# One table of times for attention, gates and out-product, and logits with a map in each half of the rows

## The chip, the core and the metric

The kernel runs on one core of a Trainium2 chip. Such a core has TensorE (PE, matrix products; its loads of weights are listed apart as PEld), VectorE (DVE), ScalarE (ACT), GpSimd (POOL) and SyncE (SP, which here only issues DMAs). Data lies in DRAM, in SBUF (128 partitions) or in PSUM (128 partitions in banks of 512 float32, where products are summed). The metric is the device time of one launch in microseconds (us).

## What is computed

The reference is one layer of an encoder over 1024 rows of width 1024, batch 1, in float32. The two groups of heads share one input projection; their results, side by side, go through one output projection, and an MLP follows.

```python
h = rms(x, norm1_g[l])
p = h @ w_in[l]
...
mix_a = mlstm_group(qk_m, v, o, gates, gate_b[l], mlstm_norm_g[l])   # 4 heads x 128
mix_b = diff_attention_group(qa, ka, va, ...)                        # 4 heads, 2 maps x 64
x = x + concat(mix_a, mix_b) @ w_out[l]
u = square(relu(rms(x, norm2_g[l]) @ w_ff1[l]))
x = x + u @ w_ff2[l]
```

Group A ends with its gate: `sigmoid(o) * hs`, where `o` is a projection of h and hs the normed scan. Group B is differential attention, with two maps of 64 dimensions for each head:

```python
q = rms(q, q_g) * 64**-0.5; k = rms(k, k_g)        # per map m = 0, 1
logits[m] = q[m] @ k[m].T + bias                     # T5 relative bias
pr = softmax(logits)
a = pr[0] - lam * pr[1]                              # 1024 keys
out = rms(a @ v, sub_g) * (1 - lam_init)
```

## The kernel before

Products that need more than one rounding are split: a float32 operand becomes a high part (`hi`, the copy by ACT in the type fp32r) and a low part (`lo`, the rest, by DVE or POOL), and `mm3` adds up three matmuls (lines 158 to 160): hi x hi, lo x hi, hi x lo. A full matmul here is 128 rows deep and 512 columns wide and fills one PSUM bank.

The program goes through stages: projections, the mLSTM of group A (its order on PE, DVE, ACT and POOL is written out by a table `O` of times, in units of work on PE: each piece of code is put on a heap with a time, and the pieces are recorded in the order of their times), then attention, the output projection, and the MLP. The change concerns the attention stage and what runs beside it.

Attention goes through 32 items. An item is one head and one block of 128 queries; the first 16 items are the first half of the rows (4 heads x 4 blocks), the other 16 the second half. Every four items, `att_load` brings a head's q and k (POOL's queue), a row table of the bias (`toe`) and v (SP's queue). For an item, `att_logits` makes for each map a tile `pl` of 128 x 1024 in PSUM (L947); DVE adds the bias, moves it to SBUF and finds the row minimum in one instruction (the signs are turned; L952); ACT takes the exponential (L955). `att_weights` mixes the maps (L962 to L965) and turns the result on PE in eight 128 x 128 transposes into two tiles `pa` (L970), which DVE and ACT copy (L973, L975). `att_product` sums eight matmuls with v into `pav` (L985; the trace has two records for each), and ACT, POOL and DVE norm it (L987 to L991). `att_turn` turns four items at once back into columns (L998).

A pl tile has two buffers in PSUM (two banks each), `pa` two, `pav` one, and `pw`, which holds gates and out-product tiles, one.

The logits: the q of a head in SBUF has its high part in the rows 0 to 63 and again in the rows 64 to 127 (two copies, two DMAs), and the same for its low part; k has its high part in the rows 0 to 63 and its low part in the rows 64 to 127. One matmul of 128 rows thus adds two of the four terms; two matmuls (q hi, q lo) make all four, for each of two maps and two halves of the keys: eight matmuls an item.

Between the items stand two generators, taken a step at a time by `step()` at a rate: `output_gates()` (L885 on: for four heads and two halves 24 matmuls into `po`, then DVE, ACT tanh, DVE with the scan's result `mfo` read back from DRAM, ACT and POOL for the split `mm`, a store) up to item 14, and `out_product(0)` from item 18 (eight tiles `pw0` of 24 matmuls, with weights split by ACT and POOL). At item 14 the buffers of the gates are given up and those of the out-product taken. The scheduler of the framework orders the instructions of this stage on each engine: it estimates when operands and engines are free, and may put a matmul of a generator anywhere between those of an item. `mfo`, `so` and `mm` have one buffer each.

The weights of the first two gates, `raw_o`, are split inside `output_gates()`, by DVE. The half 1 of the out-product and the MLP follow behind the stage.

Of the kernel before, what the change touches and what calls it, by code (L numbers as in the profile page):

```python
# [16 lines left out]
P = 128  # L17
# [31 lines left out]
def hybrid_block_kernel(ctx: ExitStack, tc: tile.TileContext, xT, w_v, w_kg, w_c, w_va, w_qa, w_o, w_1, w_2, vec, rel, onehot, outT):  # L49
# [11 lines left out]
    k_dram = [[tc.dram_tile([2, 64, 2, HB], F32, name=f"k_dram{h}{g}") for g in range(2)] for h in range(NH)]  # L61
    q_dram = [[tc.dram_tile([64, 2, 2, HB], F32, name=f"q_dram{h}{g}") for g in range(2)] for h in range(NH)]
# [103 lines left out]
    wturn = [0]  # L166

# [156 lines left out]
    def head_turn(pool, tag, bufs, z, g, is_q):  # L324
# [5 lines left out]
        for h in range(NH):  # L330
# [219 lines left out]
    def qa_done(t, p):  # L550
# [29 lines left out]
        WV=4.86, DF=0.3, Z0=1.48, Z1=2.48, Z2=2.99, Z3=5.34,  # L580
# [28 lines left out]
    for t, x in need:  # L609
        if x in W:  # L610
            continue
        late = max(t + (O["V0"] + (x - 8) * O["WV"] if x >= 8 else 0), late)
        when(late + O["W0"], w_room, x)

        first = t + max(x - 8, 0) - 0.6
        when(min(late + O["W1"], first), w_hi, x)
        when(min(late + O["W2"], first), w_lo, x)

# [266 lines left out]
    def output_gates():  # L885
        for h in range(NH):
            whi, wlo = wsplit(w_c[8 + h], f"o{h}", nc.vector if h < 2 else nc.gpsimd)
            for g in range(2):
                sl = slice(g * HB, (g + 1) * HB)
                p = psB.tile([P, HB], F32, tag="pw", name=f"po{h}{g}")  # L890
                for k in range(KT):
                    kt = slice(k * P, (k + 1) * P)
                    mm3(p, whi[:, kt], wlo[:, kt], hhi[k][:, sl], hlo[k][:, sl], k == 0, k == KT - 1)
                    if k == 3:
                        yield
                mf = spool.tile([P, HB], F32, tag="mf", name=f"mfo{h}{g}")
                loaded[0] = nc.sync.dma_start(mf, mf_dram[h][g]).ins
                so = spool.tile([P, HB], F32, tag="so", name=f"so{h}{g}")
                nc.vector.tensor_tensor(so, p, rb[:, sl], op=ALU.mult)
                nc.scalar.activation(so, so, AF.Tanh, scale=0.5)  # L900
                nc.vector.scalar_tensor_tensor(so, so, 1.0, mf, op0=ALU.add, op1=ALU.mult)
                mm = spool.tile([P, 2, HB], F32R, tag="mm", name=f"mm{h}{g}")
                nc.scalar.activation(mm[:, 0], so, AF.Copy)
                nc.gpsimd.tensor_tensor(mm[:, 1], so, mm[:, 0].bitcast(F32), op=ALU.subtract)
                nc.gpsimd.dma_start(mx_dram[h][g], mm.bitcast(F32))
                yield

# [12 lines left out]
    def att_load(it):  # L920

        h, half, hd = it.h, it.half, it.head
        hd.q = tpool.tile([P, 2, 2, HB], F32R, tag="q", name=f"q{half}{h}", bufs=2)
        for r in range(2):
            nc.gpsimd.dma_start(hd.q[r * 64 : r * 64 + 64], q_dram[h][half])
        hd.kk = tpool.tile([P, 2, S], F32R, tag="kk", name=f"kk{half}{h}", bufs=2)
        for g in range(2):
            nc.gpsimd.dma_start(
                hd.kk[:, :, g * HB : (g + 1) * HB], k_dram[h][g].rearrange("i p m t -> (i p) m t")
            )  # L930
        hd.toe = tpool.tile([P, NTOE], F32, tag="toe", name=f"toe{half}{h}", bufs=2)
        first = h * 2048 + 128 * (4 - 4 * half)
        nc.sync.dma_start(hd.toe, bass.AP(tensor=bt_dram.tensor, offset=bt_dram.offset + first, ap=[[1, P], [1, NTOE]]))
        hd.v = tpool.tile([P, NC, P], F32, tag="v", name=f"v{half}{h}", bufs=2)
        nc.sync.dma_start(hd.v, va_dram[:, :, h * P : (h + 1) * P].rearrange("c p v -> p c v"))

    def att_logits(it):

        h, qi, qb, hd = it.h, it.qi, it.qb, it.head
        it.sm = sm = tpool.tile([P, 8], F32, tag="sm", name=f"sm{qb}{h}", bufs=4)  # L940
        it.l = []
        for m in range(2):
            pl = psB.tile([P, S], F32, tag="pl", name=f"pl{qb}{h}{m}", bufs=2)
            for i in range(2):
                for kh in range(2):
                    sl = slice(kh * HB, (kh + 1) * HB)
                    nc.tensor.matmul(  # L947
                        pl[:, sl], hd.q[:, m, i, qi * P : (qi + 1) * P], hd.kk[:, m, sl], start=i == 0, stop=i == 1
                    )
            lt = tpool.tile([P, S], F32, tag=f"l{m}", name=f"l{qb}{h}{m}", bufs=3)  # L950
            off = 128 * (3 - qi)
            nc.vector.tensor_tensor_reduce(  # L952
                lt, pl, hd.toe[:, off : off + S], 1.0, 3.0e38, ALU.add, ALU.min, sm[:, m : m + 1]
            )
            nc.scalar.activation(lt, lt, AF.Exp, bias=sm[:, m : m + 1], scale=-1.0, accum_out=sm[:, 2 + m : 3 + m])  # L955
            it.l.append(lt)

    def att_weights(it):

        h, qb, sm = it.h, it.qb, it.sm  # L960
# [3 lines left out]
        a = it.l[0]  # L964
        nc.vector.scalar_tensor_tensor(a, it.l[1], rc, a, op0=ALU.mult, op1=ALU.add)  # L965
        it.ats = []
        for j2 in range(2):
            pa = psB.tile([P, HB], F32, tag="pa", name=f"pa{qb}{h}{j2}", bufs=2)
            for j in range(4):
# [116 lines left out]
    for _ in range(5):  # L1086
        step()
# [638 lines left out]
```

## Time and profile before

| What | Value |
|---|---|
| median of 3 runs | 1325.01 us (1322.83 to 1330.72) |
| profiled execution, its own time | 1329.64 us |
| its span in the profile | 1327.8 us |
| mean granted clock of PE in it | 0.984 |
| the attention stage in it | 372 to 647 us |

The profiled execution lies 4.63 us above the median of the runs. All times of single instructions come from it. In the profile a busy time is the sum over an engine's instructions; a wait is put down to the instruction whose end released it ("PE pl L947 <- DVE sm L952" reads: PE, at line 947, waited for DVE at line 952). PEclk, the granted clock, is a share of PE's full speed.

### The profile page before, as it was taken

The page shows a single profiled execution, that of the slowest core. Times are in us where ns is not written, and L with a number is a line of the kernel's source. Part 1 is how long each engine was busy: PE and PEld are TensorE (multiplying, and loading weights), DVE is VectorE, ACT ScalarE, POOL GpSimd, SP SyncE. Part 2 cuts the span into 40 slices and gives each one's busy share as a digit, 9 for nine tenths or more (in the row PEclk, how much of TensorE's full clock was granted, in tenths as well). Part 3 has the DMA queues.
Part 4 walks back from the last instruction along what each step waited for, and adds up shares of the span by engine and source line. Part 5 has one row for each costly group of instructions (what it writes and reads, how often), then busy time and mean ns, then how long its engine had stood idle before and what let it go on. Part 6 is the DMA issues. An engine that isn't in the chain of part 4 may idle for free.

```text
span 1327.8 us, 16889 instructions
## 1 busy us (share of the span) xinstructions
PE 1275.1 (96%) x6315; PEld 1056.1 (80%) x6315; DVE 857.4 (65%) x1159; ACT 605.2 (46%) x1033; POOL 281.4 (21%) x281
## 2 busy tenths in 40 slices
PE   8999989998978998999989999999999999999998
PEld 7898667887867887788878688888887888888887
DVE  7534447886327786777467888666665585458754
ACT  5323426775525555555335455445444343333332
POOL 6532312463225345442100000000000000005001
PEclk9999899999999999999999899999999999999999
DMA  6404354454196568551634476345337955344632
GB/s 210 161 24 143 69 153 102 119 134 127 49 288 165 149 209 255 160 137 49 235 138 143 147 242 231 119 153 170 127 118 263 367 182 203 120 151 159 209 132 88
DMA packets 102865, 212.49 MB, mean 160 GB/s; under 512 B 9072, under 2 KB 22128, under 8 KB 101760
## 3 DMA queue, kind: packets, MB, share of 16 engines
q1 hardware_dynamic: 78368, 154.50, 36.4%
q0 software_dynamic: 8128, 25.43, 7.1%
q10 hardware_dynamic: 16288, 31.50, 6.8%
q8 instruction: 49, 0.80, 0.3%
q14 instruction: 32, 0.26, 0.1%
HBM read 153.10 MB, written 58.29 MB: 159 GB/s over the span
## 4 chain that ended last, share of the span: by engine, by line
PE 49%; DVE 5%; ACT 1%; issue 1%; DMA 0%; POOL 0%; ACTq 0%; DVEq 0%; POOLq 0%
PE z L1568 8%; PE z L1566 8%; PE z L1567 8%; PE m L1237 7%; PE m L1238 7%; PE m L1239 7%; PE pw L160 1%; PE pw L158 1%; PE pw L159 1%; PE pav L985 1%; DVE y L1439 1%; ACT l L955 0%; PE pl L947 0%; DMA re<-in_w_dram 0%; PE pa L970 0%
## 5 line engine op out<-in xcount | busy, mean ns | idle before, releaser
L1604 POOL TENSOR_TENSOR zx<-zx,res 128x512 f32<-128x512 f32 x4 | 8.7, 2179 | 504.6 <-DVE zx L1602 504.6
L955 ACT ACTIVATE l<-l,sm 128x1024 f32<-128x1024 f32 x64 | 73.2, 1145 | 60.8 <-DVE sm L952 60.6
L1568 PE MATMUL z<-wbh,wa0l 128*128 128x512 f32 x224 | 87.4, 390 | 0.6 <-DVE wa0l L1157 0.6
L1566 PE MATMUL z<-wbh,wa0h 128*128 128x512 f32 x224 | 87.2, 389 | 0.0
L1568 PE MATMUL z<-weh,wa1l 128*128 128x512 f32 x224 | 87.2, 389 | 0.0
L1567 PE MATMUL z<-wel,wa1h 128*128 128x512 f32 x224 | 87.1, 389 | 0.0
L1567 PE MATMUL z<-wbl,wa0h 128*128 128x512 f32 x224 | 87.1, 389 | 0.0
L1566 PE MATMUL z<-weh,wa1h 128*128 128x512 f32 x224 | 87.1, 389 | 0.0
L952 DVE CUSTOM_DVE_ANT_0 l<-pl,toe 128x1024 f32<-128x1024 f32 x64 | 76.1, 1219 | 4.0 <-PE pl L947 2.2
L947 PE MATMUL pl<-kk,q 128*128 128x512 f32 x256 | 70.3, 412 | 6.9 <-DVE sm L952 6.7
L1286 ACT ACTIVATE sq<-sq 128x512 f32<-128x512 f32 x48 | 30.3, 632 | 91.8 <-DVE sq L1325 69.0
L1157 DVE TENSOR_TENSOR wel<-g,weh 128x1024 fp32r<-128x1024 f32 x28 | 35.2, 1258 | 56.5 <-ACT weh L1154 56.5
L985 PEld LDWEIGHTS pav<-v,at 128*128 128x128 f32 x512 | 62.5, 196 | 11.4 <-DVE at L973 4.9
L1157 DVE TENSOR_TENSOR wbl<-g,wbh 128x1024 fp32r<-128x1024 f32 x28 | 35.4, 1264 | 56.0 <-ACT wbh L1154 56.0
L1154 ACT ACTIVATE weh<-g 128x1024 fp32r<-128x1024 f32 x28 | 29.7, 1060 | 90.2 <-PE z L1568 53.4
L1154 ACT ACTIVATE wbh<-g 128x1024 fp32r<-128x1024 f32 x28 | 29.7, 1061 | 89.9 <-PE z L1568 52.6
L985 PE MATMUL pav<-v,at 128*128 128x128 f32 x512 | 65.5, 282 | 5.2 <-DVE at L973 3.0
L947 PEld LDWEIGHTS pl<-kk,q 128*128 128x128 f32 x256 | 46.9, 193 | 16.7 <-DVE sm L952 7.3
L160 PE MATMUL pw<-mix,lo_wo 128*128 128x512 f32 x128 | 51.8, 404 | 4.6 <-DVE lo_wo L134 4.6
L158 PE MATMUL pj_c<-hhi,hi_c 128*128 128x512 f32 x128 | 54.2, 423 | 0.0
L158 PE MATMUL pw<-mix,hi_wo 128*128 128x512 f32 x128 | 53.0, 414 | 0.2
L159 PE MATMUL pw<-mix,hi_wo 128*128 128x512 f32 x128 | 51.4, 401 | 0.0
(454 smaller groups left out, 3720.7 us busy)
## 6 DMA issues: line engine op xcount, KB each, us to landing
g<-g_dram SPq DMA_DIRECT2D x56, 512.0 KB, 4.1
g_dram<-gs SPq DMA_DIRECT2D x64, 256.0 KB, 4.5
g_dram<-sq ACTq DMA_DIRECT2D x42, 256.0 KB, 2.1
q<-q_dram POOLq DMA_DIRECT2D x16, 512.0 KB, 6.5
kk<-k_dram POOLq DMA_DIRECT2D x16, 512.0 KB, 7.2
raw_wo<-in_w_o_dram SPq DMA_DIRECT2D x16, 512.0 KB, 4.6
re<-in_w_dram SPq DMA_DIRECT2D x16, 512.0 KB, 4.4
ro<-in_w_dram SPq DMA_DIRECT2D x16, 512.0 KB, 3.5
```

Of the source, the lines that this page charges most:

```text
L158: nc.tensor.matmul(out, ahi, bhi, start=start, stop=False)
L947: nc.tensor.matmul(pl[:, sl], hd.q[:, m, i, qi * P : (qi + 1) * P], hd.kk[:, m, sl], start=i == 0, stop=i == 1)
L952: nc.vector.tensor_tensor_reduce(lt, pl, hd.toe[:, off : off + S], 1.0, 3.0e38, ALU.add, ALU.min, sm[:, m : m + 1])
L955: nc.scalar.activation(lt, lt, AF.Exp, bias=sm[:, m : m + 1], scale=-1.0, accum_out=sm[:, 2 + m : 3 + m])
L985: nc.tensor.matmul(pav[:, 0:P], at, it.head.v[:, c], start=c == 0, stop=c == NC - 1)
L1157: nc.vector.tensor_tensor(dst[1][idx], src, dst[0][idx].bitcast(F32), op=ALU.subtract)
L1237: nc.tensor.matmul(p, wh, xh, start=go, stop=False, skip_group_check=True)
L1238: nc.tensor.matmul(p, wh, xl, start=False, stop=False, skip_group_check=True)
L1239: nc.tensor.matmul(p, wl, xh, start=False, stop=stop and k == 3, skip_group_check=True)
L1566: nc.tensor.matmul(p, wh, gh, start=go, stop=False, skip_group_check=True)
L1567: nc.tensor.matmul(p, wh, gl, start=False, stop=False, skip_group_check=True)
L1568: nc.tensor.matmul(p, wl, gh, start=False, stop=end, skip_group_check=True)
```

## The change

It has two parts.

The first is the layout of the logits. q and k of a head now lie with map 0 in the rows 0 to 63 and map 1 in the rows 64 to 127, the high and the low part one behind the other in each row. They are written to DRAM by one DMA of 512 KB instead of two of 256 KB, and q is read once instead of twice. A matmul is now 64 rows deep: for each half of the keys three terms (hi x hi, lo x hi, hi x lo; the product of the low parts is left out), each for map 0 in the upper and for map 1 in the lower half of PE's rows, in turn: twelve matmuls an item. The two maps write to two `pl` tiles, which are both taken when an item's logits begin.

The second is the order. The stage is now recorded from one table `A` with times in units of one item, for PE, DVE, ACT, POOL and SP's queue. The functions of an item are cut into pieces (logits with bias, exponential, weights, transposes, copies, product, square, root, norm, turn, and the loads of q, k, `toe` on one time and v on another). The gates become pieces `gate_unit`, with halves of twelve matmuls one item apart, and the half 0 of the out-product becomes pieces `out_tile`. The split of the first two gate weights moves into the table `O` of the mLSTM stage. `out_product` keeps only the half 1.

```diff
-    k_dram = [[tc.dram_tile([2, 64, 2, HB], F32, name=f"k_dram{h}{g}") for g in range(2)] for h in range(NH)]
-    q_dram = [[tc.dram_tile([64, 2, 2, HB], F32, name=f"q_dram{h}{g}") for g in range(2)] for h in range(NH)]
+    k_dram = [[tc.dram_tile([P, 2, HB], F32, name=f"k_dram{h}{g}") for g in range(2)] for h in range(NH)]
+    q_dram = [[tc.dram_tile([P, 2, HB], F32, name=f"q_dram{h}{g}") for g in range(2)] for h in range(NH)]
...
-            for m in range(2):
-                nc.scalar.dma_start(
-                    dst[h][g][:, m] if is_q else dst[h][g][:, :, m, :].rearrange("i p t -> p i t"),
-                    zz[m * 64 : m * 64 + 64].bitcast(F32),
-                )
+            nc.scalar.dma_start(dst[h][g], zz.bitcast(F32))
...
+    rows_at = begin_at[11]
+    for h in range(2):
+        for x, f in (("R", g_room), ("H", g_hi), ("L", g_lo)):
+            when(rows_at + O[f"G{x}{h}"], f, h)
...
-        hd.q = tpool.tile([P, 2, 2, HB], F32R, tag="q", name=f"q{half}{h}", bufs=2)
-        for r in range(2):
-            nc.gpsimd.dma_start(hd.q[r * 64 : r * 64 + 64], q_dram[h][half])
+        hd.q = tpool.tile([P, 2, HB], F32R, tag="q", name=f"q{half}{h}", bufs=2)
+        nc.gpsimd.dma_start(hd.q, q_dram[h][half])
...
-            for i in range(2):
-                for kh in range(2):
-                    sl = slice(kh * HB, (kh + 1) * HB)
-                    nc.tensor.matmul(
-                        pl[:, sl], hd.q[:, m, i, qi * P : (qi + 1) * P], hd.kk[:, m, sl], start=i == 0, stop=i == 1
-                    )
...
+            it.pl = [psB.tile([P, S], F32, tag="pl", name=f"pl{qb}{h}{x}", bufs=2) for x in range(2)]
+            for kh in range(2):
+                sl = slice(kh * HB, (kh + 1) * HB)
+                for n, (i, j) in enumerate(((0, 0), (1, 0), (0, 1))):
+                    for x in range(2):
+                        r = slice(x * 64, x * 64 + 64)
+                        nc.tensor.matmul(
+                            it.pl[x][:, sl], hd.q[r, i, qi * P : (qi + 1) * P], hd.kk[r, j, sl], start=n == 0, stop=n == 2
+                        )
...
-    pending.append(output_gates())
...
-        step()
-        if 1 < n < 34:
-            att_weights(items[n - 2])
...
+    order.enter_context(tc.manual_schedule(engines={E.PE, E.DVE, E.Activation, E.Pool, E.SP}))
+    A = dict(
+        G0=-0.05, G1=0.219, E0=0.984, E1=1.396, W=1.626, A0=2.667, A1=2.819, C0=2.714, C1=2.824, P=3.534, SQ=3.666,
...
+        when(t + A["PX"], room)
+        when(t, part, 0)
+        when(t + s, part, 4)
+        when(t + s + A["PE"], out)
+        when(t + s + A["PT"], gate)
+        when(t + s + A["PB"], both)
...
+        when(t, part, 0)
+        when(t + A["OS"], part, 4)
+        when(t + A["OS"] + A["OE"], add)
...
+    while table:
+        t, _, f, args = heapq.heappop(table)
+        f(*args)
```

Three places show the new order. The first is the beginning of the stage on SP's queue: the loads of gate weights (`raw_o`), of the scan's results (`mfo`), and of item 0's `toe` and v. Before:

```order
L131 DMA raw_o_3606<-in_w_c_dram 128x1024
L131 DMA raw_o_3954<-in_w_c_dram 128x1024
L897 DMA mfo_3326<-mf_dram_82 128x512
L933 DMA toe_3291<-bt_dram 128x1408
L935 DMA v_3293<-va_dram 128x8x128
L897 DMA mfo_3361<-mf_dram_83 128x512
L933 DMA toe_3430<-bt_dram 128x1408
```

Now:

```order
L926 DMA toe_3288<-bt_dram 128x1408
L931 DMA v_3290<-va_dram 128x8x128
L1141 DMA mfo_3292<-mf_dram_82 128x512
L1141 DMA mfo_3322<-mf_dram_83 128x512
L1141 DMA mfo_3357<-mf_dram_84 128x512
L1105 DMA raw_o_3391<-in_w_c_dram 128x1024
L926 DMA toe_3435<-bt_dram 128x1408
```

v, which is read from `va_dram`, has moved ahead of the first `mfo`, and the third and fourth gate weights behind the third.

The second place is DVE at the same time, with the gates of the first two units (`so`) and item 0's minimum (`l`, `sm`). Before:

```order
L899 TENSOR_TENSOR so_3328<-po_3301,rb 128x512
L901 SCALAR_TENSOR_TENSOR so_3328<-so_3328,mfo_3326 128x512
L899 TENSOR_TENSOR so_3363<-po_3336,rb 128x512
L901 SCALAR_TENSOR_TENSOR so_3363<-so_3363,mfo_3361 128x512
L952 ISA l_3396,sm_3390<-pl_3391,toe_3291 128x1024
```

Now:

```order
L1145 TENSOR_TENSOR so_3319<-po_3294,rb 128x512
L1149 SCALAR_TENSOR_TENSOR so_3319<-so_3319,mfo_3292 128x512
L1145 TENSOR_TENSOR so_3354<-po_3324,rb 128x512
L950 ISA l_3374,sm_3359<-pl_3360,toe_3288 128x1024
L950 ISA sm_3359 128x1
L950 ISA l_3389,sm_3359<-pl_3361,toe_3288 128x1024
L950 ISA sm_3359 128x1
L1149 SCALAR_TENSOR_TENSOR so_3354<-so_3354,mfo_3322 128x512
```

Item 0's minimum has moved ahead of the second unit's multiplication with `mfo`, and stays behind the first unit's. On PE, the 48 matmuls of the first two gate units stand ahead of item 0's logits.

The third place is PE between the last gate and the first out-product tile (`pw`), in the items 12 to 18. Before:

```order
L947 MATMUL pl_4348<-kk_3947,q_3944 128x512 x4
L947 MATMUL pl_4356<-kk_3947,q_3944 128x512 x4
L970 MATMUL pa_4389<-ident,l_4185 128x128 x4
L158 MATMUL pw_4550<-mix_4309,hi_wo_4319 128x512
L159 MATMUL pw_4550<-mix_4309,hi_wo_4319 128x512
L970 MATMUL pa_4396<-ident,l_4185 128x128 x4
L970 MATMUL pa_4438<-ident,l_4266 128x128 x4
L970 MATMUL pa_4445<-ident,l_4266 128x128
L985 MATMUL pav_4364<-v_3952,at_4338 128x128 x4
L985 MATMUL pav_4364<-v_3952,at_4345 128x128 x4
```

Now (the last two rows stand six times in turn):

```order
L986 MATMUL pav_4143<-v_3799,at_4086 128x128 x4
L986 MATMUL pav_4143<-v_3799,at_4094 128x128 x4
L972 MATMUL pa_4162<-ident,l_3964 128x128 x4
L972 MATMUL pa_4171<-ident,l_3964 128x128 x4
L945 MATMUL pl_4179<-kk_3969,q_3967 128x512
L945 MATMUL pl_4180<-kk_3969,q_3967 128x512
```

An item is now product, transposes and logits, always in this order. In the six steps from item 12 to 18 no matmul of `pw` stands between them; elsewhere twelve matmuls of `po` or `pw` follow the logits in one piece. Behind the stage, from the half 1 of the out-product on, the order on every engine is as before.

More of the change, by code (lines that the diff above doesn't have):

```diff
@@ new lines, in item_pieces, with on @@
+    def item_pieces(n, it):
+        def on(name, f, *args):
+            when(n + A[name], f, it, *args)
+        if n % 4 == 0:
+            when(n + A["LD"] if n else -98.0, att_load, it)
+            when(n + A["LV"] if n else -97.0, att_load_v, it)
+        for m in range(2):
+            on(f"G{m}", att_logits, m)
+            on(f"E{m}", att_exp, m)
+            on(f"A{m}", att_across, m)
+            on(f"C{m}", att_copy, m)
+        on("W", att_weights)
+        on("P", att_product)
+        on("SQ", att_square)
+        on("RS", att_root)
+        on("ON", att_unit)
+        if n % 4 == 3 and n < 31:
+            V = {}
+            when(n + A["TU"], att_turn, items[n - 3 : n + 1], V)
+            when(n + A["TH"], att_hi, it, V)
+            when(n + A["TL"], att_lo, it, V)
@@ L1120, in hybrid_block_kernel @@
+    gate_pieces()
+    when(A["SW"], swap)
+    first_half()
+    for n, it in enumerate(items):
+        item_pieces(n, it)
+    last = {}
+    while table:
+        t, _, f, args = heapq.heappop(table)
+        f(*args)
+    order.close()
     load_mix(1)
```

286 lines of the change are left out of this document (169 added, 117 removed).

## The prediction

> **What bounds the kernel now.** I read the page first, for the span and the share of each engine.
>
> ```profile
> span 1327.8 us, 16889 instructions
> PE 1275.1 (96%) x6315; PEld 1056.1 (80%) x6315; DVE 857.4 (65%) x1159; ACT 605.2 (46%) x1033; POOL 281.4 (21%) x281
> ```
>
> PE is busy for 96% of the span and no other engine comes near it, so time is won only by giving PE less to do or by closing its gaps. The change touches one stage, the attention with the gates and half of the out-product, which the timeline puts at 372 to 647 us. The second view is therefore a table of stretches of that stage. Its columns are the stretch, its length, the busy time of PE, PEld, DVE, ACT and POOL with instructions, PE's granted clock, the DMA share and GB/s.
>
> ```profile
> 372.00:385.00 13.00, 12.22 (x55) 9.46 (x53) 1.53 (x3) 4.46 (x7) 3.49 (x5) 1.00 1.09 328
> 385.00:412.00 27.00, 20.43 (x88) 16.36 (x88) 14.79 (x24) 10.60 (x18) 8.15 (x11) 0.87 0.70 202
> 412.00:433.00 21.00, 17.54 (x95) 14.72 (x95) 14.98 (x27) 9.68 (x19) 10.07 (x14) 0.92 0.75 198
> 433.00:491.00 58.00, 57.56 (x354) 49.59 (x353) 45.79 (x83) 31.80 (x68) 21.93 (x40) 1.00 0.57 161
> 491.00:547.00 56.00, 48.90 (x290) 39.63 (x288) 39.10 (x71) 30.45 (x60) 28.46 (x40) 0.97 0.86 252
> 547.00:647.00 100.00, 96.47 (x583) 82.98 (x584) 72.27 (x124) 50.97 (x101) 32.77 (x52) 1.00 0.41 124
> sum 275.00, PE 253.11 PEld 212.75 DVE 188.46 ACT 137.95 POOL 104.86; mean PE 42.19 PEld 35.46 DVE 31.41 ACT 22.99 POOL 17.48
> ```
>
> PE stands idle for 275 - 253.1 = 21.9 us here, half of the 1327.8 - 1275.1 = 52.7 us of the whole span. The clock is below 1 in three stretches: (1 - 0.87) x 27 + (1 - 0.92) x 21 + (1 - 0.97) x 56 = 6.9 us. Together 28.8 us is what an order without any gap could win. The third view, PE's waits in the same stretch (us in total, times, longest), says what the gaps are.
>
> ```profile
> PE pl L947 <- DVE sm L952: 6.7, 2, 6.4
> PE pa L970 <- ACT at L975: 3.9, 3, 2.4
> PE pav L985 <- DVE at L973: 3.0, 1, 3.0
> PE pt L998 <- DVE on L991: 2.9, 3, 1.7
> ```
>
> They are waits for evictions that came late on an engine that was itself not full, so these are gaps of order, not of capacity.
>
> **The change, part one: the order.** A dense stretch shows what one item (128 queries of one head) costs PE when nothing waits. The columns are the start, the length, and the operation.
>
> ```profile
> 583.86 2.09 PE L947 MATMUL pl<-kk,q 128*128 128x512 f32 x8
> 585.79 1.95 PE L985 MATMUL pav<-v,at 128*128 128x128 f32 x16
> 587.50 0.47 PE L158 MATMUL pw<-mix,hi_wo 128*128 128x512 f32 x1
> 590.33 1.03 PE L970 MATMUL pa<-ident,l 128*128 128x128 f32 x8
> 591.12 2.10 PE L947 MATMUL pl<-kk,q 128*128 128x512 f32 x8
> ```
>
> Matmuls overlap, so I take distances of starts: logits 1.93, product 1.71, twelve matmuls of the out-product 2.83 (0.236 each), transposes 0.79; together 7.26 us. DVE's work for the same item is in the groups of the stage (count, then busy and mean ns of one).
>
> ```profile
> L952 DVE CUSTOM_DVE_ANT_0 l<-pl,toe 128x1024 f32<-128x1024 f32 x64 | 76.1, 1219 | 4.0 <-PE pl L947 2.2 <-DVE on L991 0.5
> L965 DVE SCALAR_TENSOR_TENSOR l<-l,sm,l 128x1024 f32<-128x1024 f32 x32 | 42.7, 1333 | 0.9
> L973 DVE COPY at<-pa 128x512 f32<-128x512 f32 x32 | 21.8, 683 | 2.8 <-PE pa L970 2.8
> L991 DVE TENSOR_SCALAR on<-pav,sm 128x128 f32<-128x128 f32 x32 | 11.2, 349 | 28.2 <-POOL sm L89 28.2
> L963 DVE TENSOR_SCALAR sm<-sm,cst 128x1 f32<-128x1 f32 x32 | 8.6, 271 | 1.0
> ```
>
> That is 2 x 1.22 + 1.33 + 0.68 + 0.35 + 0.27 = 5.07 us, under 7.26 where an item has its twelve matmuls of gate or out-product beside it. The new table gives nearly every item such a group, in one piece. Where it does, I take the gaps to close. Two places of the new order keep gaps.
>
> The first is the start. The gate's chain runs over these rows: the wait and the load of v on SP's queue, the late gate on DVE, the two halves of the split on ACT and POOL, and the sizes and landing times of three loads.
>
> ```profile
> SPq L935 <- DMA va_dram<-z: 14.9, 2, 13.4
> 384.94 0.37 SPq L935 DMA_DIRECT2D v<-va_dram  x1
> 395.27 0.69 DVE L901 SCALAR_TENSOR_TENSOR so<-so,mfo 128x512 f32<-128x512 f32 x1 [9.72 <-DMA mfo<-mf_dram]
> 380.79 0.63 ACT L903 ACTIVATE mm<-so 128x512 fp32r<-128x512 f32 x1 [1.30 <-DVE so L901]
> 381.51 1.28 POOL L904 TENSOR_TENSOR mm<-so,mm 128x512 fp32r<-128x512 f32 x1 [11.97 <-ACT mm L903]
> mfo<-mf_dram SPq DMA_DIRECT2D x8, 256.0 KB, 4.9
> q<-q_dram POOLq DMA_DIRECT2D x16, 512.0 KB, 6.5
> raw_o<-in_w_c_dram SPq DMA_DIRECT2D x4, 512.0 KB, 3.8
> ```
>
> DVE waits 9.72 us for mfo, and item 0's minimum stands behind it; PE's 6.4 us wait is that one. In the new order the first mfo stands behind v on SP, and v waits until va_dram is written. The write competes with 328 GB/s of other traffic. Two gate weights (2 x 0.5 MB) move behind the mfo loads and q is one copy instead of two (0.5 MB less), so 1.5 MB are out of the way: 1.5 MB / 328 GB/s = 4.6 us. So v starts at about 384.9 - 4.6 = 380.3, mfo lands 4.9 + 0.4 later at 385.6, and the chain adds 0.69 + 0.63 + 1.28 + 0.69 = 3.3: PE may go on at 388.9. PE has 48 gate matmuls (11.2 us) and item 0's logits (1.8) from the stage's start at 372 on, to about 385.1. That leaves 3.8 us idle, and I add 2 for a low clock behind it, as the second stretch shows one: 6.
>
> The second is items 12 to 18. The gates have run out, the out-product has not begun, and nothing lies between one item and the next. PE then needs 1.77 (worked out below) + 1.71 + 0.79 = 4.27 us per item, DVE 5.07: PE waits 0.8 six times, 5 us. All of an item's logits now need both psum tiles free, so PE can't run ahead of DVE there. Other stages show what a written table leaves.
>
> ```profile
> 165.00:373.00 208.00, 197.31 (x1093) 166.90 (x1092) 134.32 (x173) 118.05 (x305) 76.06 (x61) 0.98 0.43 116
> 690.00:1327.00 637.00, 630.12 (x2739) 513.23 (x2737) 417.21 (x484) 269.55 (x348) 24.18 (x13) 0.99 0.51 174
> ```
>
> They have 10.7 idle in 208 us and 6.9 in 637, which for 275 us is 14 and 3. My 6 + 5 = 11 lies between; bounds of what stays are 3 and, if nothing closes, 28.8. The order gives 28.8 - 11 = 17.8.
>
> **Part two: the logits.** Before, an item has 8 matmuls with 128 rows, the high and low part of k stacked. Now it has 12 with 64 rows: three terms instead of four (low times low is left out), two maps, two halves of the keys. The two maps take turns in the upper and the lower half of the rows and write to different psum banks. No row of before shows two row halves at work together. The nearest rows are a small tile of 32 rows among full ones.
>
> ```profile
> 167.30 0.40 PE L160 MATMUL pj_c<-hhi,lo_c 128*128 128x512 f32 x1
> 167.62 0.65 PE L372 MATMUL pbt<-oh,rts 32*32 32x512 f32 x2
> 168.20 0.50 PE L158 MATMUL pj_c<-hhi,hi_c 128*128 128x512 f32 x1
> 168.54 0.40 PE L159 MATMUL pj_c<-hlo,hi_c 128*128 128x512 f32 x1
> ```
>
> From 167.30 to 168.54 are four matmuls in 1.24 us, where four full ones at 0.233 take 0.93. So a small matmul costs what a full one does, and the way into another tile size and back costs 0.31 us for both. If the two halves run at once, the logits are six steps: X = 6 x 0.233 + 0.31 + about 0.06 for the second of a pair = 1.77 instead of 1.93, a gain of 0.16 x 32 = 5.1 us. If the change of size costs nothing, X = 1.40 and the gain is 17. If one half waits for the other, X = 12 x 0.233 + 0.37 = 3.17 and 32 x 1.24 = 39.7 are lost. I take the first: 64 rows leave the other half of the array free, and successive matmuls use different halves, weights and banks. The Trainium skill (TensorEngine Tiling, Key Properties) says that different tiles can load weights and multiply in parallel, and that a change of tiling mode drains TensorE; the 0.31 us agrees with the second, and no run of before shows the first.
>
> **Part three: the rest, at nothing.** One DMA of 512 KB on ACT's queue in place of two of 256 KB moves the same bytes. The split of two gate weights moves to the end of the mLSTM stage's table, on the same engines and at nearly the same place; DVE is idle there (1.53 us busy in the first stretch's 13), and if that cover is gone it is two instructions. Splits of gates and of out-product stay on POOL, which is busy 104.9 of 275 us. Behind the stage the order is the same on every engine.
>
> **The sum.** 17.8 + 5.1 = 22.9, so 1329.6 (the profiled execution) becomes 1306.7. This execution lies 4.6 us above the median of the runs, 1325.0; taken off, the forecast is **1302 us**, a ratio of 0.983.
>
> **The rivals.**
>
> First, the halves run one after the other, so that the row halves don't do what they are for. For it speaks that a 32-row matmul costs a full one's time and that nothing before shows an overlap. PE then gets 39.7 us more; the gap of items 12 to 18 vanishes (3.17 + 1.71 + 0.79 = 5.67 is above DVE's 5.07), so 6 us of gaps stay: 1325 - (28.8 - 6) + 39.7 = 1342, **slower**. The point from which it decides is X = 2.5: then 32 x 0.57 = 18 eats the order's gain. Chance 0.18.
>
> Second, the gaps stay. The waits for evictions are only moved: mfo now stands behind v on SP, gate chains have one buffer, and a table holds an engine at a wait even if something behind it could go. Against it: 433 to 491 us shows the same mix at 57.56 of 58 busy. If 24 of the 28.8 us stay, the gain is 4.8 + 5.1 = 9.9: 1315. Chance 0.20.
>
> Third, the halves overlap only in part, because each matmul needs its own weights loaded. The row is
>
> ```profile
> L947 PEld LDWEIGHTS pl<-kk,q x256: 186/188/337, 384.4 to 622.9; 128*128 128x128 f32 x128
> ```
>
> and 12 loads at 0.188 make X = 2.26 + 0.37 = 2.63, a loss of 0.70 x 32 = 22.4. With 7 us of gaps left that is 1325 - 21.8 + 22.4 = 1326. For it: each pair needs two loads. Against it: a load may be shorter with half the rows. Chance 0.12. The Trainium skill (TensorE: Matmul & The Clock Gate, Part 3) says that loads overlap running matmuls only of other row groups, which speaks for this rival; the page's rows here, with PE 96% and PEld 80% busy, show loads under matmuls of the same full tile. The same section measured 3.07 times for four 32-row tiles; at that share of the ideal an estimate by this page is X = 6 x 0.303 + 0.37 = 2.19, and the sum would be 1316.
>
> **How the numbers follow.** My forecast has a chance of 0.50; its own range is 1288 to 1312 (X = 1.40 with 9 us of gaps left below, X = 1.95 with 16 above). About 1% is what a measurement of this kernel can tell from no change, so faster means below 1311.8 and slower above 1338.3. Faster: 0.48 of the forecast's 0.50 and 0.06 of the second rival's 0.20, 0.54. Slower: 0.16 of the first rival, 0.01 of the third, 0.17. Within 1%: the remaining 0.29. The range goes from 1285, where gaps of 3 us and X = 1.50 meet, to 1335, which takes in the second and third rivals and leaves out most of the first.
>
> **What would show it.** In the new profile the start of an item's first logits to the start of its next work should be near 1.77 us in the dense part; 2.6 or 3.2 mean the third or the first rival. The two matmuls of a pair should start almost together. PE should be idle some 4 us at 385 to 389 behind mfo, and 0.8 us per item in items 12 to 18, with the minimum on DVE as releaser; between items elsewhere there should be no gap above 0.5 us. More than 15 us idle in the stage means the second rival. From the out-product's second half on, the distances should equal those of before. I am wrong if X is above 2.2, if SP's v starts later than 384, or if the fillers' groups themselves wait for splits on POOL.

## The result and the profile after

The changed kernel takes 1289.95 us in the median of four runs (1289.83 to 1292.14); the kernel before took 1324.55 us on the same chip (1322.83 to 1330.72). The ratio is 0.9735, with a 95% interval from 0.9701 to 0.9768. The forecast was 1302 us: right in sign and inside its range, 12 us too cautious.

The page of the changed kernel's profile begins so:

```profile
span 1290.4 us, 17143 instructions
PE 1257.0 (97%) x6443; PEld 1038.3 (80%) x6443; DVE 860.0 (67%) x1159; ACT 603.5 (47%) x1033; POOL 272.6 (21%) x273
```

The span is 37.4 us shorter; PE's busy time has fallen by 18.1 of these, and its idle time by the other 19.3, from 52.7 to 33.4. To see where, I read the start of the same work in both traces: the first matmul of the mLSTM's state (`pd`) at 212.0 before and 206.2 now, the first gate matmul (`po`) at 372.2 and 362.3, the first matmul of the MLP (`m`) at 697.6 and 660.8. So 5.8 us were won by the first mark, 4.1 between it and the attention, 26.9 in the attention and out-product, 0.6 behind. The forecast had 22.9 us, all in the attention.

The next view is the table of stretches of the attention in the changed kernel (columns as before: stretch, length, busy PE, PEld, DVE, ACT, POOL, PEclk, DMA share, GB/s).

```profile
362.30:376.30 14.00, 13.22 (x64) 9.88 (x61) 3.30 (x4) 5.36 (x8) 1.88 (x2) 1.00 0.55 178
376.30:455.00 78.70, 78.70 (x508) 64.38 (x507) 63.78 (x112) 43.98 (x88) 30.99 (x48) 1.00 0.58 186
455.00:489.00 34.00, 28.99 (x220) 24.29 (x219) 29.34 (x53) 21.16 (x44) 18.48 (x31) 0.95 0.75 252
489.00:609.00 120.00, 119.34 (x796) 100.24 (x795) 94.61 (x163) 66.91 (x135) 43.50 (x70) 1.00 0.50 163
sum 246.70, PE 240.25 PEld 198.79 DVE 191.03 ACT 137.41 POOL 94.84; mean PE 60.06 PEld 49.70 DVE 47.76 ACT 34.35 POOL 23.71
```

PE is busy all of the 78.7 us behind the start and 119.34 of 120 us at the end. What is left is one stretch, 455 to 489 us, the items without a filling group: 5.0 us idle and 1.7 of a lower clock. PE's waits in it (us in total, times, longest) are these.

```profile
PE pav L986 <- DVE on L1001: 2.9, 3, 1.5
PE pav L986 <- DVE mix L1017: 1.6, 1, 1.6
PE pt L1008 <- DVE on L1001: 0.6, 1, 0.6
```

Most are for the norm `on`, behind which the single `pav` buffer comes free. None is for the minimum, which I had named as the releaser. The start, where I expected PE to wait 3.8 us for a chain behind `mfo`, has only 0.78. The timeline of ACT's and SP's queues, PE and DVE there:

```profile
365.04 0.33 ACTq L845 DMA_DIRECT2D va_dram<-z  x1
...
367.25 0.36 SPq L931 DMA_DIRECT2D v<-va_dram  x1
367.66 12.06 SPq L1141 DMA_DIRECT2D mfo<-mf_dram  x3
...
368.91 0.50 PE L158 MATMUL po<-hhi,hi_o 128*128 128x512 f32 x1 [0.78 <-DVE so L1145]
...
372.26 0.69 DVE L1149 SCALAR_TENSOR_TENSOR so<-so,mfo 128x512 f32<-128x512 f32 x1 [3.40 <-DMA mfo<-mf_dram]
```

v starts 2.2 us after the last write of `va_dram` was issued (9.95 before, from 374.99 to 384.94), and `mfo` is used 4.6 us behind its issue. The gate's chain ended at 375.02, while PE was on item 0's logits (374.70 to 376.29), so the next gate matmul did not wait.

An item in the dense part now looks like this (start, length, operation):

```profile
503.48 1.04 PE L972 MATMUL pa<-ident,l 128*128 128x128 f32 x8
504.45 1.66 PE L945 MATMUL pl<-kk,q 64*128 64x512 f32 x12
506.04 0.51 PE L158 MATMUL pw<-mix,hi_wo 128*128 128x512 f32 x1
506.39 0.40 PE L159 MATMUL pw<-mix,hi_wo 128*128 128x512 f32 x1
506.62 0.40 PE L160 MATMUL pw<-mix,lo_wo 128*128 128x512 f32 x1
...
508.93 1.95 PE L986 MATMUL pav<-v,at 128*128 128x128 f32 x16
510.71 1.04 PE L972 MATMUL pa<-ident,l 128*128 128x128 f32 x8
```

Twelve matmuls of the logits take 1.59 us from the first start to the start of the next work, so they cannot run one behind the other. But the second full matmul behind them starts 0.35 us after the first instead of 0.23, and the eight transposes ahead of them take 0.97 to the next start, where they took 0.79.

### The profile page after: what moved, and what is told of

The parts are those of the page before. It is cut to its first block, busy times and chain, and to the rows that moved or that the text cites. A ratio compares the mean times of both kernels' runs of the same rounds, so it can differ in the third digit from the quotient of the medians.

```text
span 1290.4 us, 17143 instructions
## 1 busy us (share of the span) xinstructions
PE 1257.0 (97%) x6443; PEld 1038.3 (80%) x6443; DVE 860.0 (67%) x1159; ACT 603.5 (47%) x1033; POOL 272.6 (21%) x273
## 4 chain that ended last, share of the span: by engine, by line
PE 83%; DVE 8%; DMA 3%; issue 2%; ACT 2%; POOL 1%; SPq 0%; DVEq 0%; ACTq 0%; POOLq 0%
PE z L1707 8%; PE z L1705 8%; PE z L1706 8%; PE m L1376 7%; PE m L1377 7%; PE m L1378 7%; PE pav L986 4%; PE pl L945 3%; PE pv L235 3%; PE pw L158 2%; PE pa L972 2%; PE pw L160 2%; PE pw L159 2%; PE pj_c L158 2%; PE pj_c L159 2%
## 5 line engine op out<-in xcount | busy, mean ns | idle before, releaser
L945 PE MATMUL pl<-kk,q 64*128 64x512 f32 x384 | 53.3, 408 | 0.0
L159 PE MATMUL pj_c<-hlo,hi_c 128*128 128x512 f32 x128 | 50.7, 396 | 0.0
```

The costliest lines, as they stand in the source:

```text
L159: nc.tensor.matmul(out, ahi, blo, start=False, stop=False)
L945: nc.tensor.matmul(it.pl[x][:, sl], hd.q[r, i, qi * P : (qi + 1) * P], hd.kk[r, j, sl], start=n == 0, stop=n == 2)
```

## The experiments

**The order alone.** The logits go back to the old layout and the eight matmuls of 128 rows; the table stays.

```diff
-                for n, (i, j) in enumerate(((0, 0), (1, 0), (0, 1))):
-                    for x in range(2):
-                        r = slice(x * 64, x * 64 + 64)
-                        nc.tensor.matmul(
-                            it.pl[x][:, sl], hd.q[r, i, qi * P : (qi + 1) * P], hd.kk[r, j, sl], start=n == 0, stop=n == 2
-                        )
...
+                        nc.tensor.matmul(
+                            it.pl[x][:, sl], hd.q[:, x, i, qi * P : (qi + 1) * P], hd.kk[:, x, sl], start=i == 0, stop=i == 1
+                        )
```

> The changed kernel with the old logits (old layout, two q copies, 8 matmuls of 128 rows), the new order kept. If the new order carries the gain and the two row halves run at once, only 32 x (1.93 - 1.78) = 4.8 us of the logits come back: 1295 us, with X near 1.93 and the stage's idle time at or below the 7 us of the changed kernel. If the merged DMAs (one instead of two when q and k are written, one copy of q) carry part of the gain, the start of the stage and the stretch ahead of it also grow again, by 5 to 10 us: 1300 to 1305.

Measured: 1303.64 us (1297.98 to 1304.71), ratio to before 0.9823 (0.979 to 0.9857). The second branch of the expectation, in the time. In the trace the stage from the first `po` to the MLP's first matmul takes 299.7 us, against 325.4 before and 298.5 in the changed kernel: the order is worth 25.7 us and the logits 1.2 by these single executions. The attention starts at 372.4 us, as before. The two stages, up to the end of the out-product's first half (this kernel, then the changed one):

```profile
372.40:629.60 257.20, 251.80 (x1492) 218.68 (x1490) 191.85 (x331) 138.80 (x275) 98.07 (x158) 0.99 0.70 199
362.30:617.50 255.20, 248.75 (x1619) 205.81 (x1617) 191.78 (x331) 138.79 (x275) 94.84 (x151) 0.99 0.56 184
```

Where the logits stand, the changed kernel is 2.0 us shorter. Behind that mark it loses 0.8 again (43.3 us at a granted clock of 0.92, here 42.5 at 0.96), where the order is the same. The same item as above, in the order alone:

```profile
499.89 1.04 PE L978 MATMUL pa<-ident,l 128*128 128x128 f32 x8
500.68 2.10 PE L951 MATMUL pl<-kk,q 128*128 128x512 f32 x8
...
505.38 1.95 PE L992 MATMUL pav<-v,at 128*128 128x128 f32 x16
507.17 1.04 PE L978 MATMUL pa<-ident,l 128*128 128x128 f32 x8
```

From transposes to transposes it needs 7.28 us (499.89 to 507.17), the changed kernel 7.23 (503.48 to 510.71). The row halves win 0.34 us in the logits (1.93 to 1.59) and give back 0.18 ahead of them and 0.10 in the filling group behind: 0.06 an item remain.

**The logits alone.** The kernel before with the new layout and the new matmuls in `att_logits`, its scheduler kept.

```diff
+        it.pl = [psB.tile([P, S], F32, tag="pl", name=f"pl{qb}{h}{x}", bufs=2) for x in range(2)]
+        for kh in range(2):
+            sl = slice(kh * HB, (kh + 1) * HB)
+            for n, (i, j) in enumerate(((0, 0), (1, 0), (0, 1))):
+                for x in range(2):
...
-            pl = psB.tile([P, S], F32, tag="pl", name=f"pl{qb}{h}{m}", bufs=2)
+            pl = it.pl[m]
```

> The kernel before with the new layout and the new logits (12 matmuls of 64 rows), the scheduler's order kept. If the logits are worth 5 us wherever they stand: 1319 us. If the merged DMAs are worth 5 to 10 us as well: 1310 to 1315. If the scheduler breaks the twelve matmuls into pieces among full ones, so that the change of tile size is paid several times an item, or if both psum tiles free at once make PE wait more, the gain is gone: 1324 or above.

Measured: 1318.92 us (1314.56 to 1323.52), ratio 0.9953 (0.9931 to 0.9975). The time fits the first branch, but not for its reason: the stage takes 325.0 us, 0.4 less than before; the rest came ahead of it. From the first `pbt` to the first `pd` this kernel needs 49.7 us, the kernel before 59.3, the order alone 58.7. That stretch holds the writes of q, so the next question was what of it.

**The writes cut in two again.** The changed kernel; only the 512 KB write becomes two.

```diff
-            nc.scalar.dma_start(dst[h][g], zz.bitcast(F32))
+            for m in range(2):
+                nc.scalar.dma_start(dst[h][g][m * 64 : m * 64 + 64], zz[m * 64 : m * 64 + 64].bitcast(F32))
```

> The changed kernel with each 512 KB write of q and k cut into two writes of 256 KB again, in the new layout; nothing else. The scheduler then orders the projections ahead of the attention on PE, DVE and ACT as in the kernel before. If the merged write, with the order it brings, is what starts the attention stage 10 us earlier, the stage starts near 372 us again instead of 362 and the time is 1299 us. If the layout or the reads matter instead: 1290.

Measured: 1296.62 us (1295.3 to 1297.97), ratio 0.9769 (0.9739 to 0.9799). 6.7 us of the median come back, with nothing else changed (4.5 by the two ratios, since the kernel before had a median of 1328.79 us beside this run and 1324.55 beside the changed kernel's). The time lies between the two branches, and so does the start of the stage, at 366.2 us instead of 372 or 362. Behind it is this, on ACT. First the kernel before, then this variant, then the changed kernel, which has the single write:

```profile
178.78 2.83 ACTq L348 DMA_DIRECT2D q_dram<-zzTrue  x4
181.72 0.69 ACT L148 ACTIVATE zzTrue<-pzTrue,cst 128x512 fp32r<-128x512 f32 x1 [3.18 <-issue]
```

```profile
178.07 2.81 ACTq L349 DMA_DIRECT2D q_dram<-zzTrue  x4
180.98 0.69 ACT L148 ACTIVATE zzTrue<-pzTrue,cst 128x512 fp32r<-128x512 f32 x1 [3.15 <-issue]
```

```profile
177.91 1.01 ACTq L348 DMA_DIRECT2D q_dram<-zzTrue  x2
178.97 0.69 ACT L148 ACTIVATE zzTrue<-pzTrue,cst 128x512 fp32r<-128x512 f32 x1 [1.29 <-PE pzTrue L334]
```

Four issues hold ACT for 2.8 us, two for 1.0, and its next eviction stands behind them. DVE's part of the split stands behind that eviction, and PE waits for DVE: 3.2 us for `pzTrue` (the PSUM tile that this split empties) here and 1.6 in the changed kernel, and 2.8 and 0.4 for ACT's copy of k. Besides, the scheduler, which orders the projections ahead, put PE's, DVE's and ACT's instructions there in another order once ACT had fewer DMAs; this variant has the order of the kernel before. The same work on PE, `pbt` to `pd`, in the kernel before, this variant and the changed kernel:

```profile
152.70:212.00 59.30, 52.94 (x217) 38.31 (x217) 26.70 (x32) 19.50 (x33) 11.99 (x11) 0.91 0.60 145
```

```profile
153.30:210.50 57.20, 49.85 (x218) 36.90 (x218) 26.76 (x32) 19.10 (x31) 12.57 (x11) 0.97 0.57 151
```

```profile
156.00:206.20 50.20, 48.18 (x220) 36.36 (x220) 27.51 (x28) 18.96 (x28) 14.86 (x12) 1.00 0.60 178
```

With the single write PE is idle 2.0 us there (50.20 - 48.18) instead of 6.4 and 7.4, and the clock stays at 1. This stretch takes 49.7 to 50.2 us in all ten kernels here with the single write and 57.2 to 59.3 in the three with two. The next one, from `pd` to the first gate matmul, takes 155.7 us here, 156.1 in the changed kernel, and 159.0 to 160.2 in the eleven others, most of which have the same code there as the changed kernel: this difference is one of executions, not of the change. How the 6.7 us divide between fewer issues and the other order was not tried apart.

**The old matmuls with the merged writes.** As the order alone, but q and k lie in DRAM as in the changed kernel and are read into the old places in smaller pieces.

```diff
+        for r in range(2):
+            nc.gpsimd.dma_start(hd.q[r * 64 : r * 64 + 64], q_dram[h][half].rearrange("(m p) i t -> p m i t", m=2))
...
+            for i in range(2):
+                nc.gpsimd.dma_start(
+                    hd.kk[i * 64 : i * 64 + 64, :, g * HB : (g + 1) * HB],
+                    k_dram[h][g].rearrange("(m p) i t -> i p m t", m=2)[i],
+                )
```

> The changed kernel with the old matmuls of the logits (8 of 128 rows, four terms), but with the merged writes kept: q and k lie in DRAM as in the changed kernel and are read into the old places by smaller reads (k in four of 256 KB a head instead of two of 512 KB, q in two). If the row halves themselves bring only some 1 us in the stage, as order_only and logits_only show, and the merged write the rest: 1291 to 1293, with the stage starting near 362 to 364. If the halves are worth the 5 us that I predicted: 1295 or above.

Measured: 1299.79 us (1296.93 to 1301.47), ratio 0.9808 (0.9773 to 0.9843): the second branch in the time, though not because the matmuls are worth 5 us. The stage starts at 362.7 us, as expected; it takes 303.7 us, 4.0 more than with the whole reads, and PE has extra gaps of 2.40 us at 379.46, behind the gate's chain on DVE, and of 1.16 us at 401.32, for k. So this run shows the start again, and does not price the matmuls, since the smaller reads have a cost of their own.

**Three by three, six by six, and all in one half.** Three kernels ask how the halves work together. In the first the three matmuls of map 0 stand ahead of the three of map 1 for each half of the keys, in the second all six ahead of all six, in the third both maps use the same rows.

```diff
-                for n, (i, j) in enumerate(((0, 0), (1, 0), (0, 1))):
-                    for x in range(2):
-                        r = slice(x * 64, x * 64 + 64)
+                for x in range(2):
+                    r = slice(x * 64, x * 64 + 64)
+                    for n, (i, j) in enumerate(((0, 0), (1, 0), (0, 1))):
```

> The changed kernel with the same twelve matmuls an item, but for each half of the keys first the three of map 0, then the three of map 1. If the halves only run at once when neighbours in the queue use different halves, ten of the twelve run alone or nearly so: X is 2.6 to 3.1 instead of 1.78, 32 x 0.8 to 1.3 = 26 to 42 us, less some 4 us of gaps in items 12 to 18 that close: 1312 to 1328. If the order of the halves doesn't matter: 1290.

> The changed kernel with the six matmuls of map 0 first and the six of map 1 behind them. Three by three still started in pairs, so something looks past three matmuls of the busy half. If it looks past six: pairs, 1.59 us, 1290. If it looks past about four only, one or two pairs less start together: 1.8 to 2.4 us, 1295 to 1315.

```diff
-                        r = slice(x * 64, x * 64 + 64)
+                        r = slice(0, 64)
```

> The changed kernel with map 1 computed from the rows 0 to 63 like map 0, so that all twelve matmuls of an item lie in the same half of PE's rows (map 1's logits are then those of map 0). If two halves run at once, this takes the overlap away: the matmuls start 0.23 us apart, the logits take 1.59 + 6 x 0.233 = 2.99 us to the next start, 32 x 1.4 = 45 us more, less some 5 us of gaps that close in items 12 to 18: 1330. If a matmul of 64 rows is simply shorter: 1290.

Measured, one run each: 1294.8 us three by three, 1306.51 six by six, 1333.42 in one half. The median distance from an item's first logits to the next work (ten items that are followed by the gate) is 1.59, 2.16 and 2.95 us. In one half, the timeline of PE shows it as follows.

```profile
388.21 3.01 PE L945 MATMUL pl<-kk,q 64*128 64x512 f32 x12
391.15 0.50 PE L158 MATMUL po<-hhi,hi_o 128*128 128x512 f32 x1
```

2.94 us, as worked out from twelve steps, and 43 us in the whole: a matmul of 64 rows is not shorter, the overlap of the halves is the whole of the gain. Three by three is the same as in turn (the stage takes 299.0 us against 298.5), which was the less expected branch. Six by six, four pairs overlap instead of six: map 1's first matmul starts beside map 0's third, 0.58 us behind the first (median), map 1's first four run beside map 0's last four, and its last two run alone. Each of these three times is a single run; the order of the starts comes from its trace.

**The start with its old traffic.** The loads of the third and fourth gate weights, 1 MB, go back ahead of `toe` and v.

```diff
-        when(max(t + A[pre + "W"], floor), room)
+        when(-98.5 if pre == "P" else max(t + A[pre + "W"], floor), room)
```

> The changed kernel with the loads of the third and fourth gate weights (1 MB) put back ahead of toe and v at the stage's start, as before. If the start is now smooth because the write of va_dram no longer stands behind other traffic, v starts 8 to 10 us behind that write instead of 2.2, DVE waits 8 us or more for the first mfo instead of 3.4, and PE is idle 4 to 6 us there: 1294 to 1297. If the order of mfo and the minimum on DVE made the difference, not the traffic: within 1 us of 1290.

Measured: 1297.33 us (1296.91 to 1302.03), ratio 0.9783 (0.9752 to 0.9815). The timeline of SP's queue, DVE and PE:

```profile
372.25 0.35 SPq L1105 DMA_DIRECT2D raw_o<-in_w_c_dram  x1
...
373.27 0.38 SPq L931 DMA_DIRECT2D v<-va_dram  x1
373.74 14.97 SPq L1141 DMA_DIRECT2D mfo<-mf_dram  x3
...
382.05 0.69 DVE L1149 SCALAR_TENSOR_TENSOR so<-so,mfo 128x512 f32<-128x512 f32 x1 [8.70 <-DMA mfo<-mf_dram]
...
385.52 0.80 PE L158 MATMUL po<-hhi,hi_o 128*128 128x512 f32 x1 [4.67 <-DVE so L1145]
386.12 0.63 PE L159 MATMUL po<-hlo,hi_o 128*128 128x512 f32 x1
```

The stage takes 303.3 us, 4.8 more. PE waits 4.67 us and then goes at steps of 0.43 to 0.6 us instead of 0.23, at a granted clock of 0.54 (385.5 to 390 us). The gap has the size that was expected, but it came another way. v starts 3.7 us behind the last write of `va_dram` (issued at 369.53), not 8 to 10. SP's queue stood at the fourth gate weight until 372.25, when DVE had freed its buffer, and then the first `mfo` was used 8.3 us behind its issue instead of 4.6, with that weight, `toe` and v in flight. So the loads decide this gap, and not where the minimum stands on DVE, which is as in the changed kernel; that they hold up the write of `va_dram` is not shown by this run.

**The fillers spread.** Six intervals in a row lack a filling group. Three kernels spread them: the gate's halves 1.2 items apart; or 1.015 apart with two, or with three, intervals skipped. The change of buffers moves to 16.3, 15.3 and 16.4.

```diff
-        RS=3.676, ON=3.783, TU=4.131, TH=4.141, TL=4.151, LD=-2.901, LV=-1.095, PF=-4, PS=1.015, PE=0.388, PT=1.671,
-        PB=1.957, PW=-3.566, PH=-2.613, PL=-1.973, PX=-0.258, SW=15.195, OF=18.423, OS=0.979, OE=0.323, OQ=0.587,
+        RS=3.676, ON=3.783, TU=4.131, TH=4.141, TL=4.151, LD=-2.901, LV=-1.095, PF=-4, PS=1.2, PE=0.388, PT=1.671,
+        PB=1.957, PW=-3.566, PH=-2.613, PL=-1.973, PX=-0.258, SW=16.3, OF=18.423, OS=0.979, OE=0.323, OQ=0.587,
```

> The changed kernel with the gate's halves 1.2 items apart instead of 1.015 and the change of buffers at 16.3 instead of 15.2, so that only three intervals between items lack a filling group instead of six. If the missing filler is what leaves PE idle at 455 to 489 us (5.0 us and 1.7 of a lower clock): 2 to 4 us less there, 1287. If DVE is the bound there whatever PE does, or a late group waits for its split on POOL: 1290 or above.

```diff
+        at = [A["PF"] + (u + max(0, u // 4 - 1)) * A["PS"] for u in range(16)]
+        w_at = [at[4 * h] for h in range(NH)]
...
-            gate_unit(h, g, T, w_at[h] + 2 * g * A["PS"])
+            gate_unit(h, g, T, at[4 * h + 2 * g], at[4 * h + 2 * g + 1])
```

> The changed kernel with the gate's halves still one item apart (1.015), but two single intervals between items left without a filling group at items 4 and 8, and the change of buffers at 15.3; so four intervals in a row lack a filler at items 14 to 18 instead of six at 12 to 18. If a single interval without filler costs nothing, because the dense items around it let DVE catch up, 2 x 0.8 to 1.2 us go: 1288. If each such interval costs the same wherever it lies: 1290. The version with halves 1.2 apart lost 16 us in this stage; if that came from the phase of the pieces and not from where the gaps lie, nothing of it shows here.

With three, the times skip one step more:

```diff
-        at = [A["PF"] + (u + max(0, u // 4 - 1)) * A["PS"] for u in range(16)]
+        at = [A["PF"] + (u + max(0, (u + 1) // 4 - 1)) * A["PS"] for u in range(16)]
```

> As two_skips, with three single intervals without filler and the change of buffers at 16.4, so that three in a row remain. If spreading is what counts: 1287. The out-product's first weights and mix are then loaded 2.0 items ahead of their first matmul instead of 3.2; if that is too little, PE waits there for the split on POOL or for mix, 3 us or more: 1292 or above.

Measured: 1310.6 us (1308.91 to 1316.72), ratio 0.9887 (0.9843 to 0.9932), with 1.2 apart; 1290.27 (1286.38 to 1292.3), 0.9727 (0.9687 to 0.9767), with two skips; 1300.57 (1298.82 to 1302.05), 0.9809 (0.9779 to 0.9839), with three. The first is a miss by 20 us. With two skips the stage takes 297.1 us, 1.4 less, but not where the fillers are: up to the end of the out-product's first half it takes 254.9 against 254.8 (to 617.9 and 617.1 us), and the rest lies behind it, at a granted clock of 0.96 against 0.92. The single intervals without filler still cost a wait of 1.34 and one of 0.76 us. No version beat the changed kernel by more than its interval. Three skips show what the late change of buffers does, in the timeline of POOL, DVE and PE:

```profile
487.37 2.14 POOL L1025 DMA_DIRECT2D mix<-mx_dram  x4
489.47 2.41 POOL L1112 TENSOR_TENSOR lo_wo<-raw_wo,hi_wo 128x1024 fp32r<-128x1024 f32 x1
491.98 0.27 POOL L993 TENSOR_SCALAR sm<-sm 128x1 f32<-128x1 f32 x1
...
493.19 0.35 DVE L1001 TENSOR_SCALAR on<-pav,sm 128x128 f32<-128x128 f32 x1 [4.16 <-POOL sm L89]
...
493.60 3.78 PE L986 MATMUL pav<-v,at 128*128 128x128 f32 x16 [4.83 <-DVE on L1001]
```

DVE waited 4.16 us for a small root on POOL, `pav`'s only bank stayed taken, and PE waited 4.83; the sixteen records of the product then took 3.78 us instead of 1.95. POOL came to the root's pieces (from 491.98) only after it had issued the four loads of `mix`, 2.14 us, and split a weight of the out-product, 2.41 us. The rows show this order; a kernel with the split elsewhere was not tried. I had expected the wait at the out-product's first matmul, not here. The first version has a wait of the same kind (4.6 us, `pav` for `on`), besides others where the pieces fell out of step with the items.

## Why the prediction was right, and where it was off

The time came out 12 us below the forecast and still inside the range, because errors of opposite sign met: the order and the writes brought 14.6 us more than forecast, the logits 3 to 4 us less. That the sum holds is partly luck; what held and what did not follows by terms.

- **Order, 17.8 us forecast, 25.7 shown** (order alone against before, stage 325.4 to 299.7). The mechanism held: gaps close where a filling group stands beside an item. The size was off at two places. The start was priced at 6 us and cost about 1: v starts 2.2 us behind the write of `va_dram` instead of 9.95, and 4.0 in the order alone, where q is still read twice. I had counted 1.5 MB out of the write's way; `toe` (0.7 MB) and the first `mfo` had left it too. I take that as the reason, but the loads were not tried one by one, and the gate weights put back cost 4.8 us by another way. And I counted idle time and low clock only; PE's busy time for the same 1492 matmuls in the stretch up to the out-product's end fell from 260.91 to 251.80 us, 9.1, of which the lower clock (0.98 and 0.99 granted) explains some 3 to 5. The rest I can't place.
- **Items 12 to 18, 5 us forecast, 5.0 idle measured**, but not in the way forecast. I had six waits of 0.8 us for the minimum, with DVE full. There are five waits of 0.57 to 1.56 us, for `on` and `mix`; DVE is busy 29.34 of 34 us and waits for PE in turn (1.6 us for `pl`, 1.4 for `pa`), and it has work of a gate and of `mix` there that my 5.07 us left out. DVE has a little more to do there than PE (28.99 us), as I said, but it is not full; that the sizes agree is in part luck.
- **Row halves at once: right.** All in one half cost 43 us more. This was the first rival, and it would have come true at 2.94 us an item.
- **The worth of the logits, 5.1 us forecast, 2.0 where they stand, 1.2 over the stage (0.4 without the new order).** The term that failed is the price of the change of tile size: 0.37 us with the pair, taken from two small matmuls among full ones. Here 0.18 is lost ahead, 0.10 behind, and 0.19 inside (1.59 against six steps of 0.233), 0.47 together, so X is 1.87, and the 1.93 that it was set against was right: 0.06 x 32 = 1.9 us were to be had, not 5.1, which fits the 2.0.
- **"The rest, at nothing": wrong.** The merged writes brought 6.7 us in the median (writes cut in two again), ahead of the stage that I looked at. I had counted bytes; on ACT's queue the number of issues counted (2.8 us for four, 1.0 for two), and the scheduler reordered the projections when that queue got shorter.
- **Run to run:** the profiled execution before was 4.6 us above its median, as said; of the 9.9 us ahead of the stage, the 3 that the writes leave lie within that, and the stretch behind `pd` shows such a difference between executions of the same code.
- **The second rival** (gaps only moved) did not come: 6.45 us of idle time stay in 362.3 to 609, not 15. **The third** (weight loads bind) neither: 12 loads of 0.188 would take 2.26 us, and the logits take 1.59. A load with half the rows is hardly shorter (0.184 us), so the loads of the two halves overlap too.

25.7 + 1.2 + 6.7 = 33.6 of the 34.6 us between the medians. The first two are differences of single executions and the third is one of medians, so a sum this near is not a proof. By the medians the order is worth 21.1 us with the old logits (1324.72 to 1303.64) and 29.0 with the new ones and the merged writes (1318.92 to 1289.95); in the stage it is 25.7 and 26.5. The kernel before alone spreads from 1321 to 1331 us, so the size of this term stays open by some 4 us.

## What to carry to other kernels

Price a narrow matmul with the way in and out of its tile size, per group and not per matmul: here 0.47 us a group of twelve ate most of what the two row halves won (0.53). Fewer, longer groups should pay more; that was not tried. Count DMA issues on an engine's own queue as work of that engine, and compare the built order over the whole program, not only in the stage that the change names, since a scheduler moves what lies ahead. In a table of times, a rate that doesn't fit the items is dear: stretching the fillers by 1.2 cost 20 us, where skipping two whole intervals cost nothing. Part of the 20 us may come from the late change of buffers, which cost 10.6 us with three skips; the two were not tried apart.

## What the chip showed that I had not expected

Two halves of 64 rows run at once even when three matmuls of one half stand in the queue ahead of the other's (1.59 us either way), and still in part with six (2.16, four pairs of six). So a matmul of the free half starts past waiting ones of the busy half: past two of them three by three, past three (map 0's last) six by six, and no further in these runs. Turns written out by hand are not needed at a depth of three. Four DMA issues on ACT took 2.83 us, two 1.01. And the waits of 4.67 us in the start and of 4.83 us with three skips were each followed by matmuls at about twice their usual distance, at granted clocks of 0.54 and 0.50. In the changed kernel a wait of only 1.56 us in items 12 to 18 was followed by a product of 3.48 us, so the length of one gap does not tell it alone.
